# Hymba layer on one core: five of the up stage's 258-column tiles with rows 1280 bytes apart, and a down-stage pool that opens later

## The chip, the cores and the metric

The kernel runs on one core of a Trainium2 chip. A core has five engines with their own instruction streams: TensorE (PE in the profile; its weight loads are PEld), VectorE (DVE), ScalarE (ACT), GpSimd (POOL) and SyncE (SP), which here only issues DMA transfers. They share an on-chip memory of 128 partitions (SBUF); TensorE writes its sums to a second one (PSUM) in banks of 512 float32 columns. Engines wait for each other through semaphores.

The metric is device time of one execution in microseconds, the median of several runs. Lower is better.

## The reference

The reference is one decoder layer in float32: a normalized input goes through a joint projection into differential attention and an HGRN2 recurrence, an output projection and a residual sum, and then through a convolutional feed-forward block, which is what this change touches:

```python
D_FF = 2816
CONV_WIDTH = 3

def conv_ffn(a, w_up, conv_w, conv_b, w_down):
    u = a @ w_up                                   # (1040, 1024) @ (1024, 5632)
    C = u.shape[-1]
    u = lax.conv_general_dilated(
        u, conv_w[:, None, :].astype(u.dtype), window_strides=(1,),
        padding=[(CONV_WIDTH - 1, 0)], dimension_numbers=('NWC', 'WIO', 'NWC'),
        feature_group_count=C) + conv_b
    gate, up = jnp.split(u, 2, axis=-1)
    return (jax.nn.gelu(gate, approximate=True) * up) @ w_down

def reference(...):
    ...
    for l in range(DEPTH):
        ...
        mix = jnp.concatenate([y_diff, y_hgrn], axis=-1) @ w_out[l]
        h = h + rmsnorm(mix, ln_mix_post[l])
        a = rmsnorm(h, ln_ffn_pre[l])
        y = conv_ffn(a, w_ffn_up[l], ffn_conv_w[l], ffn_conv_b[l], w_ffn_down[l])
        h = h + rmsnorm(y, ln_ffn_post[l])
    return h[:, N_META:, :]
```

## The kernel before

**Precision.** Each float32 product is made of three matmuls in a rounded format (float32r): an operand is split into `hi`, its rounded value, and `lo`, the rest, and the matmuls are hi x hi, hi x lo and lo x hi. ScalarE makes `hi` (a CAST in the profile), VectorE or GpSimd subtract it from the operand to get `lo`.

**The up stage** computes u = a @ w_up transposed: channels on the partitions, tokens along the columns. The tokens lie in two parts, p = 0 and p = 1. With the halo of the convolution a part has 516 or 512 columns, which are handled as two halves of `WN[p]` = 258 or 256. The loop `for ft in range(1, NF)` goes over 21 blocks of 128 gate channels and the 128 up channels that belong to them; the prediction calls one pass a round. Block 0 is done ahead of it by `plain_unit`.

A round is a 2 x 2 by 2 x 2 block product (channels gate and up, halves of the inner dimension, halves of the tokens) in Winograd's form: seven products instead of eight, the steps j = 0 to 6. Product j multiplies a weight combination, made anew in every round by `prep` (names `uh`, `ul` for its hi and lo, `ws` for sums on GpSimd, `ra` for the loaded weights), with a token combination, made once before the loop (`t_sums`, `t_split`, `quarter`) and kept in a tile `t0_j` or `t1_j` (the profile calls all of them `t`). A tile holds eight rows per partition: four k-slices of hi, then four of lo. Before the change they follow each other without a gap: 258 x 4 = 1032 bytes for p = 0, 1024 for p = 1. All tiles start at an address that is 32 above a multiple of 64.

`unit(ft, p, ...)` is one part of a round, written as a generator that yields after each step. Step j issues twelve matmuls, for each k-slice hi x hi, then weight-hi x token-lo, then weight-lo x token-hi (lines 1383, 1384, 1385). The loop takes step j of p = 0, then of p = 1, then the next step. TensorE's order is exactly this. The products are added into three PSUM banks: `pa` for j = 0 and 4, `pb` for j = 1, 3 and 5, `pc` for j = 2 and 6. Between two products in one bank the sum so far is read out, by ScalarE (`x`, `ug`) or by VectorE (`u`, `uu`, `ug`), and the next product waits for that read. So j = 3 waits until VectorE has formed `u` (code name `u2`) from `pb`, and j = 5 until it has formed the next `u` (`u3`).

After the last step `gated` does the convolution: per side (gate `ug`, up `uu`) ScalarE starts it (`c` = last tap plus bias), VectorE adds two taps (SCALAR_TENSOR_TENSOR), ScalarE applies gelu to the gate, GpSimd multiplies the two sides, and SyncE stores the result to DRAM (`gsc`). These run while TensorE does the next round's first steps.

The other engines' order is set by a scheduler when the kernel is built, within what the code asks for (`issue_after`). Memory is handed out by pools: a tile of a pool with a tag takes the place of the last tile with that tag, and a pool opened later takes the addresses of pools closed before; the new user waits for the last readers of the tiles that lay there.

**The token tiles' places before.** For p = 0: tiles 0 and 4 in the pool `early` (`e0`, `e1`), tiles 1, 2, 3 in `tsplit`, tile 6 in the mix pool's X1, tile 7 (used by block 0 alone) in X2, and tile 5 after it in X2. For p = 1 they lie in `tsplit`, `tsplit2` and X0.

**The down stage** computes y = g @ w_down with the same Winograd form, 11 k-steps for each of seven products. `operands` loads a block of g (`gi`) and of the weights (`wi`), or uses the loaded ones it is given, and splits them into `gh`, `gl`, `wh`, `wl`. Twelve 512-column matmuls follow per k-step (`mms`). The buffers for `gi`, `gh` and `gl`, four of each, come from the pool `down`, which before is open from the start of the up loop. The first three k-steps are prepared early: in the last round, their loads are issued at j = 1 (after the store of the round before) and their splits at j = 4, 5, 6. When the up stage's pools are closed the pool `fin` takes their place.

Of the kernel before, what the change touches and what calls it, by code (L numbers as in the profile page):

```python
# [9 lines left out]
F32 = mybir.dt.float32  # L10
F32R = mybir.dt.float32r
# [6 lines left out]
P = 128  # L18
# [6 lines left out]
NF = DFF // P  # L25
# [7 lines left out]
C0 = [0, 514]  # L33
FA, FH, FO = 840, 800, 740


# [49 lines left out]
def layer_kernel(ctx: ExitStack, tc: tile.TileContext, x, meta, table, lbl, gpre, gpost, win,  # L86
# [1161 lines left out]
    def t_tiles(p, j, where, tag):  # L1248
        tag, n = (tag + (8 * WN[p],))[:2]
        both = where.tile([P, n], F32R, tag=tag, name=f"t{p}_{j}")[:, :8 * WN[p]].rearrange("p (a c) -> p a c", a=8)  # L1250
        return both[:, 0:4], both[:, 4:8]

    def t_split(p, j, src, where, *tag):
        hi, lo = t_tiles(p, j, where, tag)
        A.copy(hi, src)
        V.tensor_tensor(lo, src, hi.bitcast(F32), op=ALU.subtract)
        tt[p][j] = (hi, lo)
# [6 lines left out]
    def t_sums(p, where, last):  # L1264
# [4 lines left out]
        for j, b in ((1, b22), (2, b11), (3, b12)):  # L1269
            t_split(p, j, b, where, f"t{p}_{j}")  # L1270
        V.tensor_tensor(b21, b21, b22, op=ALU.subtract)
# [150 lines left out]
    t_split(1, 6, quarter(1, 6), mxp, "X0", MIX["X0"])  # L1422
    t_sums(0, tp, (mxp, "X2", MIX["X2"]))
    close(a_cms.pop())
    t2_cm, t2p = pool("tsplit2", 1)
    gap(t2p, "gap2", 320)
    p1 = plain_unit(1, ps_b)
# [6 lines left out]
    gap(cv, "gap3", 224)  # L1434
    dn_cm, dn = pool("down", 4, "right")
    next(p0)
    for j in range(4, 7):
        prep(7 + j)
# [8 lines left out]

    def g_in(k, half, nm):
        t = dn.tile([P, 512], F32, tag="gk", name=f"gi{nm}_{k}")
        SY.dma_start(t, g_src(k, half))  # L1450
        return t
# [10 lines left out]
    def operands(pr, k, loaded=None):  # L1462
# [20 lines left out]
        nm = f"{pr}_{k}"  # L1483
        gh = dn.tile([P, 512], F32R, tag="gh", name=f"gh{nm}")
        gl = dn.tile([P, 512], F32R, tag="gl", name=f"gl{nm}")
        split(gh, gl, a, V)
# [5 lines left out]
    for ft in range(1, NF):  # L1492
        units = [unit(ft, p, ps_b) for p in range(2)]
        for j in range(7):
            prep(7 * (ft + 1) + j)
            for u in units:
                next(u)
            if (ft, j) == (1, 1):
                with tc.issue_after(marks[1, 1].ins):
                    next(p1)  # L1500
            if ft == NF - 1 and j == 1:
                with tc.issue_after(marks["store"].ins):
                    opens = [(g_in(k, 0, "1"), w_in(1, k)) for k in range(LOOK)]
            if ft == NF - 1 and j > 3:
                with tc.issue_after(marks["left"].ins):
                    ready[j - 4] = operands(1, j - 4, opens[j - 4])
    close(t2_cm, t_cm, xu_cm, mx_cm)

# [186 lines left out]
```

## Time and profile before

| what | value |
|---|---|
| median of 3 runs | 1302.69 us (1301.43 to 1303.88) |
| profiled execution, its own time | 1300.73 us |
| its span, first to last instruction | 1298.9 us |
| granted TensorE clock, mean | 0.998 |
| TensorE busy | 1268.1 us, 98% of the span |
| VectorE, ScalarE, GpSimd busy | 68%, 54%, 37% |
| up loop, first matmul to last | 656.09 to 1076.39 us |
| down stage from | 1076.50 us |

In the profile an instruction stands with its line, its engine, the operation, what it writes and reads by the program's names (without buffer numbers), and its shape. Nearly all VectorE, ScalarE and GpSimd instructions have line 53, that of a helper through which they are issued. Matmuls overlap: one lasts some 280 ns from start to end while the next starts 113 to 125 ns after it, so the pace is read from the distance of starts, not from the durations. In the timeline a row is the start in microseconds, the duration, the engine, and the instruction; "x2" are several alike in a row; in brackets stands idle time of the engine before it and what ended it. A row of a stretch has the busy time and number of instructions of PE, PEld, DVE, ACT and POOL, the granted clock, the busy share of the DMA engines and GB/s. A row of the waits has who waited for whom, the sum in microseconds, the number of times and the longest.

### The profile page before, as it was taken

Reading aid. Unit: us, or ns where it says so; the run is one execution under the profiler, and the core shown is the slowest. Engines: PE = TensorE matmul, PEld = TensorE weight load, DVE = VectorE, ACT = ScalarE, POOL = GpSimd, SP = SyncE. Lnnn points to the kernel's source line nnn. Section 1 sums busy time; section 2 is a strip of 40 time slices with the busy share of each in tenths; the row PEclk is TensorE's granted clock in tenths of the full one; section 3 lists DMA queues with packets and bytes.
Section 4 is the critical chain, followed back from the end, with each engine's and each line's share of the span. In section 5 each row is a group of like instructions: output and inputs, shape, how many; then the busy total and the mean of one; then the engine's idle time right before and its main releaser. Section 6 shows DMA issues by size and latency. Waiting matters only on the chain.

```text
span 1298.9 us, 26100 instructions
## 1 busy us (share of the span) xinstructions
PE 1268.1 (98%) x10154; PEld 1179.0 (91%) x10154; DVE 887.0 (68%) x1488; ACT 695.1 (54%) x1639; POOL 482.6 (37%) x387
## 2 busy tenths in 40 slices
PE   8999999999999999999999999999999999999996
PEld 7999999899999998767899999999999998888885
DVE  7574646465645574547897877778778767697686
ACT  8465466546654764356854544544445435554553
POOL 5231423242323310353066575666665731010121
PEclk9999999999999999999999999999999999999999
DMA  6244655182644532787312222222222128964263
GB/s 215 94 99 89 120 120 116 47 156 78 125 116 86 122 103 90 222 272 265 117 67 82 90 75 82 74 89 83 74 75 90 66 79 274 336 203 170 90 211 122
DMA packets 116418, 165.04 MB, mean 127 GB/s; under 512 B 10099, under 2 KB 57523, under 8 KB 116294
## 3 DMA queue, kind: packets, MB, share of 16 engines
q1 hardware_dynamic: 93062, 151.84, 35.1%
q0 software_dynamic: 23232, 11.54, 7.6%
q8 instruction: 80, 1.31, 0.4%
q14 instruction: 44, 0.36, 0.1%
HBM read 134.24 MB, written 52.17 MB: 144 GB/s over the span
## 4 chain that ended last, share of the span: by engine, by line
PE 46%; DVE 4%; ACT 2%; issue 1%; DMA 1%; DVEq 0%; ACTq 0%
PE pd L1544 5%; PE pd L1545 5%; PE pd L1543 5%; PE pb L1383 5%; PE pb L1384 4%; PE pb L1385 4%; PE pa L1384 3%; PE pa L1383 3%; PE pa L1385 3%; PE pc L1384 3%; PE pc L1383 3%; PE pc L1385 3%; DVE c L53 1%; DVE t L53 1%; DVE xh L53 1%
## 5 line engine op out<-in xcount | busy, mean ns | idle before, releaser
L1383 PE MATMUL pb<-t,uh 128*128 128x258 f32 x504 | 142.5, 283 | 2.9 <-DVE u L53 2.7
L1384 PE MATMUL pb<-t,uh 128*128 128x258 f32 x504 | 141.2, 280 | 0.0
L1385 PE MATMUL pb<-t,ul 128*128 128x258 f32 x504 | 141.0, 280 | 0.0
L1544 PE MATMUL pd<-wl,gh 128*128 128x512 f32 x308 | 120.5, 391 | 2.0 <-DVE wl L53 2.0
L1545 PE MATMUL pd<-wh,gl 128*128 128x512 f32 x308 | 120.0, 390 | 0.0
L1543 PE MATMUL pd<-wh,gh 128*128 128x512 f32 x308 | 120.0, 390 | 0.0
L53 DVE SCALAR_TENSOR_TENSOR c<-uu,cwt,c 128x514 f32<-128x514 f32 (+1 forms) x88 | 96.5, 1096 | 19.6 <-ACT c L53 18.9
L53 POOL TENSOR_TENSOR c<-c,c 128x514 f32<-128x514 f32 (+1 forms) x44 | 63.8, 1449 | 122.3 <-ACT c L53 120.2
L1383 PEld LDWEIGHTS pb<-t,uh 128*128 128x128 f32 x504 | 95.0, 189 | 5.3 <-DVE u L53 5.3
L1385 PEld LDWEIGHTS pb<-t,ul 128*128 128x128 f32 x504 | 95.3, 189 | 0.0
L1384 PEld LDWEIGHTS pb<-t,uh 128*128 128x128 f32 x504 | 95.0, 188 | 0.0
L1384 PE MATMUL pa<-t,uh 128*128 128x258 f32 (+1 forms) x336 | 94.7, 282 | 0.0
L1383 PE MATMUL pa<-t,uh 128*128 128x258 f32 (+1 forms) x336 | 94.6, 281 | 0.0
L1385 PE MATMUL pa<-t,ul 128*128 128x258 f32 (+1 forms) x336 | 94.3, 281 | 0.0
L1384 PE MATMUL pc<-t,uh 128*128 128x258 f32 (+1 forms) x336 | 94.1, 280 | 0.0
L1385 PE MATMUL pc<-t,ul 128*128 128x258 f32 (+1 forms) x336 | 94.1, 280 | 0.0
L1383 PE MATMUL pc<-t,uh 128*128 128x258 f32 (+1 forms) x336 | 93.9, 279 | 0.0
L53 DVE SCALAR_TENSOR_TENSOR c<-ug,cwt,c 128x514 f32<-128x514 f32 (+1 forms) x88 | 88.3, 1004 | 1.4 <-ACT c L53 0.6
L53 ACT CAST uh<-ra 128x512 fp32r<-128x512 f32 x67 | 41.1, 617 | 63.2 <-PE pb L1384 42.0
L53 DVE TENSOR_TENSOR ul<-ra,uh 128x512 fp32r<-128x512 f32 x42 | 40.2, 957 | 48.7 <-ACT uh L53 48.7
L53 POOL TENSOR_TENSOR ul<-ws,uh 128x512 fp32r<-128x512 f32 x42 | 60.4, 1437 | 34.4 <-ACT uh L53 33.7
L1544 PEld LDWEIGHTS pd<-wl,gh 128*128 128x128 f32 x308 | 57.8, 188 | 15.5 <-DVE wl L53 3.7
(388 smaller groups left out, 4167.1 us busy)
## 6 DMA issues: line engine op xcount, KB each, us to landing
ra<-in_wup_dram SPq DMA_DIRECT2D x88, 256.0 KB, 2.6
mp<-msc SPq DMA_DIRECT2D x23, 512.0 KB, 5.0
tsc<-in_wdown_dram SPq DMA_DIRECT2D x44, 256.0 KB, 4.5
wi<-tsc SPq DMA_DIRECT2D x44, 256.0 KB, 2.7
gi<-gsc SPq DMA_DIRECT2D x33, 256.0 KB, 4.4
wi<-in_wdown_dram SPq DMA_DIRECT2D x33, 256.0 KB, 5.2
gsc<-c SPq DMA_DIRECT2D x22, 257.0 KB, 2.0
tsc<-in_wdown_dram POOLq DMA_DIRECT2D x22, 256.0 KB, 7.4
```

The lines of the kernel that those rows point to most:

```text
L53: ins = call(*args, **kw)
L1383: T.matmul(pt, hi[:, s], th[:, k], start=(first and k == 0), stop=False, skip_group_check=True)
L1384: T.matmul(pt, hi[:, s], tl[:, k], start=False, stop=False, skip_group_check=True)
L1385: T.matmul(pt, lo[:, s], th[:, k], start=False, stop=(k == 3), skip_group_check=True)
L1543: T.matmul(py, gh[:, s], wh, start=(k == 0 and pr not in (3, 7)), stop=False, skip_group_check=True)
L1544: T.matmul(py, gh[:, s], wl, start=False, stop=False, skip_group_check=True)
L1545: T.matmul(py, gl[:, s], wh, start=False, stop=(k == NH - 1), skip_group_check=True)
```

## The change

`wide_tiles` makes a token tile of 8 rows of `ROW` = 320 float32 values, 1280 bytes, of which 258 are used, from column `off` on. The tiles 1, 2, 3, 5 and 6 of p = 0 become such tiles; tile 3 starts 32 columns (128 bytes) into its rows and tile 6 starts 16 (64 bytes) in. Tiles 0, 4 and 7 of p = 0 and all of p = 1 keep their rows. Tile 5 no longer takes tile 7's place but has a tag of its own in `tsplit`. Tile 6 is made in X1 as before and copied by ScalarE into a wide tile of a new pool, `tsplit3`, after the last step of block 0.

A wide tile takes 10240 bytes per partition instead of 8256. The pool `down` no longer exists during the up stage; it is opened when the up stage's tiles are gone. The three early k-steps of the down stage therefore use other places: their g loads go to `raw_g`, which takes the place of p = 1's tile 0, and their `gh` and `gl` to four rows of 512 columns in a tile that takes the place of p = 0's wide tile 1 (two k-steps) or 2 (one).

```diff
+ROW = 320
...
+    def wide_tiles(j, off, where=None):
+        both = (where or tp).tile([P, 8 * ROW], F32R, tag=f"t0_{j}", name=f"t0_{j}w")
+        both = both.rearrange("p (a c) -> p a c", a=8)[:, :, off:off + WN[0]]
+        return both[:, 0:4], both[:, 4:8]
+
     def t_split(p, j, src, where, *tag):
-        hi, lo = t_tiles(p, j, where, tag)
+        hi, lo = wide_tiles(j, where) if isinstance(where, int) else t_tiles(p, j, where, tag)
         A.copy(hi, src)
         V.tensor_tensor(lo, src, hi.bitcast(F32), op=ALU.subtract)
...
         for j, b in ((1, b22), (2, b11), (3, b12)):
-            t_split(p, j, b, where, f"t{p}_{j}")
+            t_split(p, j, b, where[j] if p == 0 else where, f"t{p}_{j}")
...
-    t_sums(0, tp, (mxp, "X2", MIX["X2"]))
+    t_sums(0, {1: 0, 2: 0, 3: 32}, (0,))
     close(a_cms.pop())
     t2_cm, t2p = pool("tsplit2", 1)
-    gap(t2p, "gap2", 320)
...
-    dn_cm, dn = pool("down", 4, "right")
+    t3_cm, t3p = pool("tsplit3", 1)
     next(p0)
+    own, tt[0][6] = tt[0][6], wide_tiles(6, 16, t3p)
+    for new, old in zip(tt[0][6], own):
+        A.copy(new, old.bitcast(F32))
...
-    def g_in(k, half, nm):
-        t = dn.tile([P, 512], F32, tag="gk", name=f"gi{nm}_{k}")
+    def g_in(k, half, nm, t=None):
+        t = dn.tile([P, 512], F32, tag="gk", name=f"gi{nm}_{k}") if t is None else t
...
-        gh = dn.tile([P, 512], F32R, tag="gh", name=f"gh{nm}")
-        gl = dn.tile([P, 512], F32R, tag="gl", name=f"gl{nm}")
+        if loaded:
+            gh, gl = loaded[2:]
+        else:
+            gh = dn.tile([P, 512], F32R, tag="gh", name=f"gh{nm}")
+            gl = dn.tile([P, 512], F32R, tag="gl", name=f"gl{nm}")
...
             if ft == NF - 1 and j == 1:
+                raw_g = tp.tile([P, 4, 512], F32, tag="t1_0", name="raw_g")
                 with tc.issue_after(marks["store"].ins):
-                    opens = [(g_in(k, 0, "1"), w_in(1, k)) for k in range(LOOK)]
+                    opens = [(g_in(k, 0, "1", raw_g[:, k]), w_in(1, k)) for k in range(LOOK)]
+            if ft == NF - 1 and j in (4, 6):
+                halves = tp.tile([P, 8 * ROW], F32R, tag=f"t0_{j // 2 - 1}", name=f"open{j}")[:, 16:2064]
+                halves = halves.rearrange("p (a c) -> p a c", a=4)
             if ft == NF - 1 and j > 3:
+                a = 2 * (j % 2)
                 with tc.issue_after(marks["left"].ins):
-                    ready[j - 4] = operands(1, j - 4, opens[j - 4])
-    close(t2_cm, t_cm, xu_cm, mx_cm)
+                    ready[j - 4] = operands(1, j - 4, opens[j - 4] + (halves[:, a], halves[:, a + 1]))
+    close(t3_cm, t2_cm, t_cm, xu_cm, mx_cm)
+    dn_cm, dn = pool("down", 4, "right")
```

TensorE's order does not change. On the other engines only a few instructions move. ScalarE in round 1, before the change (`x1_1_0` and `x1_1_1` are the reads of `pa` for the two parts, `c0` and `c1` the convolutions' starts, `uh15` to `uh17` weight casts for the next steps):

```order
L53 COPY x1_1_0_8007<-pa1_0_8010 128x258
L53 ACTIVATE c0_0_0_7966<-ug0_0_7642,cbt_85,cwt_84 128x514
L53 ACTIVATE c1_0_0_7971<-uu0_0_7643,cbt_85,cwt_84 128x514
L53 COPY x1_1_1_8026<-pa1_1_8029 128x256
L53 CAST uh15_8045<-ws2_8043 128x512
L53 ACTIVATE c0_0_1_8077<-ug0_1_7819,cbt_85,cwt_84 128x510
L53 ACTIVATE c1_0_1_8082<-uu0_1_7820,cbt_85,cwt_84 128x510
L53 ACT_TABLE_LOAD
L53 ACTIVATE c0_0_0_7966<-c0_0_0_7966 128x514
L53 CAST uh16_8088<-ws1_7999 128x512
```

and after it:

```order
L54 COPY x1_1_0_8009<-pa1_0_8012 128x258
L54 ACTIVATE c0_0_0_7965<-ug0_0_7642,cbt_85,cwt_84 128x514
L54 ACTIVATE c1_0_0_7970<-uu0_0_7643,cbt_85,cwt_84 128x514
L54 CAST t0_6w_7976<-t0_6_7575 128x4x258 x2
L54 ACT_TABLE_LOAD
L54 ACTIVATE c0_0_0_7965<-c0_0_0_7965 128x514
L54 COPY x1_1_1_8028<-pa1_1_8031 128x256
L54 CAST uh15_8047<-ws2_8045 128x512
L54 ACTIVATE c0_0_1_8079<-ug0_1_7818,cbt_85,cwt_84 128x510
L54 ACTIVATE c1_0_1_8084<-uu0_1_7819,cbt_85,cwt_84 128x510
L54 CAST uh16_8090<-ws1_8001 128x512
```

The two copies (one row, x2), the table load and the gelu of p = 0 (the ACTIVATE that reads and writes `c0_0_0`) now stand ahead of `x1_1_1`, of `uh15` and of the convolution's start for p = 1.

VectorE at the same place, before the change (`u2_1_0` and `u2_1_1` read the bank that j = 3 waits for, `ul15` is the remainder of weight `uh15`):

```order
L53 SCALAR_TENSOR_TENSOR c1_0_0_7971<-uu0_0_7643,cwt_84,c1_0_0_7971 128x514
L53 TENSOR_TENSOR ul15_8046<-ws2_8043,uh15_8045 128x512
L53 TENSOR_TENSOR u2_1_0_8008<-pb1_0_8049,x1_1_0_8007 128x258
L53 TENSOR_TENSOR u2_1_1_8027<-pb1_1_8063,x1_1_1_8026 128x256
L53 SCALAR_TENSOR_TENSOR c0_0_1_8077<-ug0_1_7819,cwt_84,c0_0_1_8077 128x510
```

and after it:

```order
L54 SCALAR_TENSOR_TENSOR c1_0_0_7970<-uu0_0_7643,cwt_84,c1_0_0_7970 128x514
L54 TENSOR_TENSOR u2_1_0_8010<-pb1_0_8051,x1_1_0_8009 128x258
L54 TENSOR_TENSOR u2_1_1_8029<-pb1_1_8065,x1_1_1_8028 128x256
L54 TENSOR_TENSOR ul15_8048<-ws2_8045,uh15_8047 128x512
L54 SCALAR_TENSOR_TENSOR c0_0_1_8079<-ug0_1_7818,cwt_84,c0_0_1_8079 128x510
```

The weight's remainder has moved behind the two `u2`.

SyncE's queue in the last round and at the start of the down stage, before the change (`gi1_k` and `wi1_k` are the loads of k-step k of the first product, `gi5_11` belongs to a later product's sums, the last row is the store of the last round's p = 0):

```order
L1450 DMA gi1_2_13356<-gsc_90 128x512
L1459 DMA wi1_2_13358<-in_wdown_dram 128x512
L1450 DMA gi1_3_13556<-gsc_90 128x512
L1459 DMA wi1_3_13558<-in_wdown_dram 128x512
L1459 DMA wi1_4_13591<-in_wdown_dram 128x512
L1450 DMA gi5_11_13569<-gsc_90 128x512
L1459 DMA wi1_5_13615<-in_wdown_dram 128x512
L1450 DMA gi1_4_13589<-gsc_90 128x512
L1459 DMA wi1_6_13639<-in_wdown_dram 128x512
L1351 DMA gsc_90<-c0_21_0_13495 128x514
```

and after it:

```order
L1458 DMA raw_g_13350<-gsc_90 128x512
L1467 DMA wi1_2_13358<-in_wdown_dram 128x512
L1467 DMA wi1_3_13558<-in_wdown_dram 128x512
L1467 DMA wi1_4_13591<-in_wdown_dram 128x512
L1467 DMA wi1_5_13615<-in_wdown_dram 128x512
L1467 DMA wi1_6_13639<-in_wdown_dram 128x512
L1458 DMA gi1_3_13556<-gsc_90 128x512
L1458 DMA gi5_11_13569<-gsc_90 128x512
L1458 DMA gi1_4_13589<-gsc_90 128x512
L1458 DMA gi1_5_13613<-gsc_90 128x512
L1357 DMA gsc_90<-c0_21_0_13492 128x514
```

The load of `gi1_3` now stands behind the weight loads up to `wi1_6`, and `gi1_5` has come ahead of the store.

## The prediction

> **What bounds the kernel now.** I read the page's head first, then busy time by stretch, then the timeline of TensorE and of VectorE over a few rounds of the up stage, then the waits. A round is one pass of the `ft` loop: seven steps j, each twice (p = 0 with 258 columns, p = 1 with 256), twelve matmuls a group.
>
> ```profile
> span 1298.9 us, 26100 instructions
> PE 1268.1 (98%) x10154; PEld 1179.0 (91%) x10154; DVE 887.0 (68%) x1488; ACT 695.1 (54%) x1639; POOL 482.6 (37%) x387
> ```
> ```profile
> 680.00:1060.00 380.00, 379.79 (x3214) 377.83 (x3214) 291.75 (x423) 183.00 (x326) 239.93 (x169) 1.00 0.22 77
> ```
>
> The second row is the steady part of the up stage: TensorE is never idle for more than moments, at a granted clock of 1.00, and VectorE is busy 77%. So a round lasts as long as its matmuls, unless someone keeps them waiting. These are first matmuls of groups in round 4 (start, duration); two neighbouring starts are the two ends of one group:
>
> ```profile
> 738.90 0.29 PE L1383 MATMUL pa<-t,uh 128*128 128x258 f32 x1
> ...
> 741.72 0.28 PE L1383 MATMUL pb<-t,uh 128*128 128x258 f32 x1
> ...
> 743.16 0.28 PE L1383 MATMUL pb<-t,uh 128*128 128x256 f32 x1
> ...
> 744.57 0.28 PE L1383 MATMUL pc<-t,uh 128*128 128x258 f32 x1
> ...
> 745.99 0.28 PE L1383 MATMUL pc<-t,uh 128*128 128x256 f32 x1
> ...
> 747.35 0.28 PE L1383 MATMUL pb<-t,uh 128*128 128x258 f32 x1
> ...
> 748.78 0.28 PE L1383 MATMUL pb<-t,uh 128*128 128x256 f32 x1
> ...
> 752.99 0.28 PE L1383 MATMUL pb<-t,uh 128*128 128x258 f32 x1
> ...
> 754.41 0.28 PE L1383 MATMUL pb<-t,uh 128*128 128x256 f32 x1
> ...
> 755.77 0.28 PE L1383 MATMUL pc<-t,uh 128*128 128x258 f32 x1
> ...
> 757.24 0.28 PE L1383 MATMUL pc<-t,uh 128*128 128x256 f32 x1
> ...
> 758.61 0.29 PE L1383 MATMUL pa<-t,uh 128*128 128x258 f32 x1
> ```
>
> The round takes 19.71 us. The 258-column groups of the five tiles in question take 1.44 (j = 1), 1.42 (j = 2), 1.43 (j = 3), 1.42 (j = 5) and 1.47 (j = 6), 7.18 together. The 256-column groups take 1.36 (j = 2 and 5) or 1.37 (j = 6), but 1.41 after tile 1. At 1.36, 113 ns a matmul, 258 columns would cost 1.36 x 258/256 = 1.37. So the 258-column groups lose 0.05 to 0.10 us each to something other than their two extra columns. What sets them apart in the code is that their rows start at every multiple of 8 bytes (1032 apart), while the 256-column rows are 1024 apart. That the same kind of 256-column group takes 1.36 or 1.41 shows a second factor: a group seems to inherit a slow or a fast pace from the one before.
>
> Every second round also has a wait at j = 3, where matmuls add into a bank that VectorE must first have read:
>
> ```profile
> 727.49 0.39 PE L1383 MATMUL pb<-t,uh 128*128 128x258 f32 x1
> ```
> ```profile
> 766.95 0.28 PE L1385 MATMUL pc<-t,ul 128*128 128x256 f32 x1
> 767.23 0.39 PE L1383 MATMUL pb<-t,uh 128*128 128x258 f32 x1
> 767.45 0.29 PE L1384 MATMUL pb<-t,uh 128*128 128x258 f32 x1
> ```
> ```profile
> PEld pb L1383 <- DVE u L53: 2.2, 10, 0.2
> ```
>
> Ten such waits; the steps 0.28 and 0.22 instead of 0.11 and 0.12 cost 0.27 us each, of which 0.10 is the restart. Two rounds so take 39.72 or so (19.86 on average) instead of 39.4. The VectorE rows of that loop:
>
> ```profile
> 734.01 0.88 DVE L53 TENSOR_TENSOR ul<-ra,uh 128x512 fp32r<-128x512 f32 x1 [2.50 <-ACT uh L53]
> 734.90 0.43 DVE L53 TENSOR_TENSOR uu<-pb,x 128x258 f32<-128x258 f32 x1
> ...
> 746.38 0.74 DVE L53 TENSOR_TENSOR u<-pb,x 128x258 f32<-128x258 f32 x2
> ...
> 753.73 1.63 DVE L53 TENSOR_TENSOR ul<-ra,uh 128x512 fp32r<-128x512 f32 x1 [2.45 <-ACT uh L53]
> 755.29 0.41 DVE L53 TENSOR_TENSOR uu<-pb,x 128x258 f32<-128x258 f32 x1
> ```
> ```profile
> 753.53 1.29 POOL L53 TENSOR_TENSOR ul<-ra,uh 128x512 fp32r<-128x512 f32 x1
> ```
>
> From `uu` (it opens the convolutions) to the `u` that frees the bank VectorE works nearly without a break: 755.29 to the matmul at 767.23 is 11.94. Before that lies the leg from j = 3 to `uu`. In round 4 it is 747.35 to 755.29, 7.94, because `ul` took 1.63 beside a GpSimd `ul`. In round 3 `ul` took 0.88; its `uu` plus 11.94 gives 746.84, and TensorE came at 747.35, so nobody waited.
>
> **The change, part by part.** *Wide rows.* Five tiles times 12 matmuls per round. No instruction is added in the round. Bounds: at best all five groups run at 1.37, saving 7.18 - 6.85 = 0.33, and the 256-column group after tile 1 goes from 1.41 to 1.36: 0.38 in all, a TensorE round of 19.33. At worst they run at the slow pace, 1.41 x 258/256 = 1.42, and pass it on (a rival, below). I take the best end: these rows become like the 256-column ones, all starting at the same remainder, and four of the seven groups of that kind in round 4 are at the fast pace after a neighbour that isn't.
>
> The Trainium skill, page "TensorE: Matmul & The Clock Gate", section "Wait — 56ns, not 53.3ns?", has warm back-to-back matmuls start every N / 2.4 GHz plus about 2.5 ns: 109 ns for 256 columns and 110 for 258, whatever the rows' distance. This trace disagrees, with 113 to 122 ns; by that rule the wide rows would save nothing.
>
> *What VectorE leaves of it.* Of the leg, the p = 0 groups j = 3 and j = 5 shrink by 0.06 and 0.05. A round with a quick `ul` then needs 7.41 (727.49 to 734.90) - 0.11 + 11.94 = 19.24: just under TensorE's 19.33. With a slow `ul` it needs 7.94 - 0.11 + 11.94 = 19.77. Slow every second round as now: (19.33 + 0.10 restart + 19.77)/2 = 19.60, a gain of 0.27 against 19.87. Every third: (19.43 + 19.33 + 19.77)/3 = 19.51, 0.36. Never: 0.54. Always: 0.10. The quick rounds now have 0.09 of slack instead of 0.51, so `ul` comes earlier against GpSimd's and hits it less often: I take between every second and every third, 0.31. Over 20 rounds (2 to 21) that is 6.2 us.
>
> *Round 1.* It is VectorE's, not TensorE's:
>
> ```profile
> PE pb L1383 <- DVE u L53: 2.7, 2, 1.4
> ```
> ```profile
> 641.75 2.97 ACT L53 CAST t<-at 128x1032 fp32r<-128x1032 f32 x3
> ...
> 660.08 0.35 ACT L53 COPY x<-pa 128x256 f32<-128x256 f32 x1
> ...
> 664.35 0.63 ACT L53 ACTIVATE c<-c 128x514 f32<-128x514 f32 x1 [0.68 <-DVE c L53]
> ```
> ```profile
> 665.51 0.74 DVE L53 TENSOR_TENSOR u<-pb,x 128x258 f32<-128x258 f32 x2
> 666.18 1.11 DVE L53 SCALAR_TENSOR_TENSOR c<-ug,cwt,c 128x510 f32<-128x510 f32 x1
> ...
> 672.89 0.41 DVE L53 TENSOR_TENSOR u<-pb,x 128x258 f32<-128x258 f32 x1
> ```
>
> So its faster groups gain nothing. The two copies of tile 6 take 1.0 each (2.97 for three). They, the table load and the gelu now stand ahead of `x` and of the second pair's convolution starts on ScalarE. The gelu still waits for VectorE until 664.3, so `x` comes at 664.9 instead of 660.1, the next weight cast ends at 665.8 and the convolution start at 666.6. VectorE's `u` for p = 0 moves ahead of a weight remainder and ends the first wait somewhat sooner, but the convolution begins at 666.6 for 666.18, and at its end stands the `u` at 672.89 for which TensorE waits: +0.4. Bounds: -0.6 (all GpSimd work that slows these convolutions moves away) to +1.0. Tile 6 is needed at j = 6, two groups after 672.89: hidden. Tile 5's own buffer ends a wait for tile 7 that no row shows: nothing.
>
> *The start of the down stage.* The first three operands lie in buffers of p = 1's tile 0 and p = 0's tiles 1 and 2, last read at j = 0, 1 and 2 of the round, before the loads and splits. The fourth load moves behind four weight loads on the queue:
>
> ```profile
> 1068.08 0.43 SPq L1450 DMA_DIRECT2D gi<-gsc  x1
> ...
> 1075.26 0.33 SPq L1459 DMA_DIRECT2D wi<-in_wdown_dram  x1
> ```
> ```profile
> gi<-gsc SPq DMA_DIRECT2D x33, 256.0 KB, 4.4
> ```
> ```profile
> 1079.44 0.64 ACT L53 ACTIVATE c<-c 128x514 f32<-128x514 f32 x1 [0.92 <-DVE c L53]
> ```
> ```profile
> 1082.96 0.68 DVE L53 TENSOR_TENSOR wl<-wi,wh 128x512 fp32r<-128x512 f32 x1
> ```
> ```profile
> 1083.69 0.50 PE L1544 MATMUL pd<-wl,gh 128*128 128x512 f32 x1 [1.34 <-DVE wl L53]
> ```
>
> It is issued after the 1075.26 row instead of at 1068.08 and lands near 1080.1. Its cast now stands ahead of the last round's first gelu, which slips by about 1.2, and with it a product and a store whose rows are read much later. Its remainder on VectorE comes after the 1082.96 row as before, so TensorE resumes at 1083.69 for the same reason. I count nothing; the cover is the 3 us from 1080.1 to 1083. If it is gone, +1.3.
>
> *Sum.* -6.2 + 0.4 = -5.8. The profiled execution took 1300.73 (span 1298.9), 1.96 under the median 1302.69, a little below the lowest shown; the difference carries over: 1302.7 - 5.8 = 1296.9.
>
> **The rivals.** *All of it kept.* No slow `ul` left: 20 x 0.54 - 0.4 = 10.4, 1292.3. For it: less slack. Against it: it needs GpSimd never in the way.
>
> *VectorE takes over.* Every round slow: 20 x 0.10 - 0.4 = 1.6, 1301.1. For it: 77% busy, and TensorE's rest shrinks. Against it: a stalled round has had a quick `ul` after it (734.01).
>
> *The slow pace spreads* (the other side). The five wide groups take 1.42, saving 0.08, and the five 256-column groups now at 1.36 or 1.37 take 1.41, losing 0.23: 0.15 x 20 + 0.4 = 3.4 more, 1306.1. For it: the 256-column group after tile 1 stays at 1.41 for all twelve matmuls though its rows never shift, so equal rows alone don't end the slow pace. Against it: the same kind of group at j = 2 and 5 is quick. It decides once two more groups a round turn slow with nothing saved elsewhere.
>
> *Nothing in the matmuls changes.* The rows' distance is not the cause; only round 1's 0.4 is left: 1303.1. The page's rule above would have it so. Against it: 1.47 for tile 6 beside 1.37 for its neighbour, which two columns don't explain.
>
> **How the numbers follow.** The forecast (1295 to 1299) 0.60, all kept 0.10, VectorE 0.10, slow pace 0.13, nothing 0.07. The time is that of the first, 1296.9. The range leaves out the slow pace and some of the ends: 1291.8 to 1303.2. About 0.2% (2.6 us) is what a measurement of this kernel can tell from no change: faster 0.73 (the first two and a third of the VectorE case), same 0.13, slower 0.14.
>
> **What would show it.** Right: the five 258-column groups at 1.37 to 1.38, the 256-column group after tile 1 at 1.36, the pace of tiles 0 and 4 unchanged, a round near 19.5, waits on `u` at j = 3 no rarer than one round in three; round 1's second wait up by 0.4; the fourth operand landing near three microseconds before its remainder starts. Wrong: groups of 1.42, or quick groups with a round still near 19.8, the rest being waits on `u`.

## The result, and the profile after

The changed kernel took 1304.38 us (median of 22 runs), the kernel before, run beside it, 1302.07 us (22 runs). The ratio is 1.0028 with a 95% interval of 1.0015 to 1.0041: slower by some 3.6 us (the ratio goes by the means, 1305.9 and 1302.1; the medians lie 2.3 apart), where 5.8 us less were forecast. The 22 times fall in two groups, 13 from 1301.1 to 1305.4 (mean 1303.3) and nine from 1307.6 to 1311.3 (mean 1309.6). No run of the kernel before is above 1306. The profiled execution, 1310.75 us by its own time, is one of the long ones, 10.0 us longer than the profiled one of before.

These rows cut the kernel before at the first up matmul, at the starts of rounds 2 and 18, and at the last up matmul (stretch and its length, then busy time and instructions of PE, PEld, DVE, ACT and POOL, the granted clock, the DMA share, GB/s):

```profile
656.09:679.10 23.01, 20.29 (x171) 19.89 (x169) 21.71 (x25) 12.90 (x22) 20.03 (x11) 1.00 0.23 81
679.10:997.04 317.94, 317.79 (x2690) 316.22 (x2689) 243.81 (x353) 152.81 (x273) 205.07 (x144) 1.00 0.23 81
997.04:1076.39 79.35, 79.29 (x673) 78.90 (x672) 58.03 (x90) 37.62 (x69) 38.32 (x27) 1.00 0.27 89
1076.39:1298.90 222.51, 210.99 (x927) 173.11 (x925) 167.29 (x243) 109.94 (x220) 26.71 (x17) 0.99 0.58 198
```

And the changed kernel at the same places:

```profile
658.86:683.71 24.85, 21.73 (x170) 21.34 (x169) 23.05 (x26) 15.01 (x24) 20.31 (x12) 0.93 0.25 85
683.71:1002.05 318.34, 318.15 (x2690) 317.02 (x2689) 243.97 (x353) 152.86 (x272) 204.93 (x145) 1.00 0.24 80
1002.05:1081.23 79.18, 79.18 (x674) 79.06 (x672) 57.90 (x89) 37.91 (x68) 37.55 (x27) 1.00 0.25 81
1081.23:1308.90 227.67, 213.49 (x927) 174.07 (x925) 165.79 (x243) 109.72 (x220) 31.63 (x17) 0.98 0.59 197
```

Between the two spans (1298.9 and 1308.9) lie 2.8 us ahead of the up stage, 1.8 in round 1, 0.4 in the sixteen rounds after it, -0.2 in the last four, and 5.2 in the down stage. The 2.8 arise ahead of 400 us, in code that the change leaves alone, and three executions of the changed kernel start their first up matmul at 656.6, 658.9 and 659.7 us (e11, this one and e10 below), so they say nothing of the change. The steady round, where the gain was to be, went from 317.94/16 = 19.87 to 318.34/16 = 19.90 us.

**The matmuls.** The starts of the groups in round 4 of the changed kernel, a round without a wait; `t_1w` to `t_6w` are the wide tiles:

```profile
726.25 0.28 PE L1389 MATMUL pb<-t_1w,uh 128*128 128x258 f32 x1
...
727.69 0.28 PE L1389 MATMUL pb<-t,uh 128*128 128x256 f32 x1
...
729.06 0.28 PE L1389 MATMUL pc<-t_2w,uh 128*128 128x258 f32 x1
...
730.51 0.28 PE L1389 MATMUL pc<-t,uh 128*128 128x256 f32 x1
...
731.88 0.28 PE L1389 MATMUL pb<-t_3w,uh 128*128 128x258 f32 x1
...
733.30 0.28 PE L1389 MATMUL pb<-t,uh 128*128 128x256 f32 x1
...
737.52 0.28 PE L1389 MATMUL pb<-t_5w,uh 128*128 128x258 f32 x1
...
738.97 0.29 PE L1389 MATMUL pb<-t,uh 128*128 128x256 f32 x1
...
740.36 0.28 PE L1389 MATMUL pc<-t_6w,uh 128*128 128x258 f32 x1
...
741.79 0.28 PE L1389 MATMUL pc<-t,uh 128*128 128x256 f32 x1
...
743.21 0.28 PE L1389 MATMUL pa<-t,uh 128*128 128x258 f32 x1
```

The wide groups take 1.44, 1.45, 1.42, 1.45 and 1.43 us, 7.19 together, where they took 7.18 with narrow rows. Single groups did move: tiles 2 and 5 lost 0.03 each and tile 6 gained 0.04. Inside tile 1's group the steps between matmuls still vary, from 114 to 125 ns as before, although every row now starts at the same remainder; tile 6's group settles at an even 120 ns after its fifth matmul. The 256-column group after tile 1 did turn quick (1.41 to 1.37), but the one after tile 6 turned slow (1.37 to 1.42). TensorE's round without a wait went from 19.71 to 19.77.

**Round 1.** TensorE's waits between 655 and 690 us (who waited for whom, the sum, the number, the longest):

```profile
PE pb L1389 <- DVE u L54: 3.1, 2, 2.4
```

Before, it was 2.7 in two waits of at most 1.4. So the sum rose by 0.4 and the longest by 1.0. These are the reads of `pb` that end the two waits, on VectorE:

```profile
667.68 0.79 DVE L54 TENSOR_TENSOR u<-pb,x 128x258 f32<-128x258 f32 x2
...
676.05 0.74 DVE L54 TENSOR_TENSOR u<-pb,x 128x258 f32<-128x258 f32 x2
```

They start 8.37 us apart, before the change 7.38 (665.51 to 672.89), and the weight's remainder that moved now stands between them: the first wait became shorter, the second longer. In the stretch row of round 1 the granted clock is 0.93 instead of 1.00: right behind the long wait, from 676.6 to 679.6 us, it is 0.50, and the matmuls start 214 ns apart instead of 119.

**The start of the down stage.** The last round's two gate products on GpSimd, before and after the change:

```profile
1080.15 1.74 POOL L53 TENSOR_TENSOR c<-c,c 128x514 f32<-128x514 f32 x1 [15.33 <-ACT c L53]
1083.23 1.55 POOL L53 TENSOR_TENSOR c<-c,c 128x510 f32<-128x510 f32 x1 [1.34 <-issue]
```
```profile
1085.42 8.42 POOL L54 TENSOR_TENSOR c<-c,c 128x514 f32<-128x514 f32 x2 [15.82 <-ACT c L54]
```

The gelu ahead of the first of them, and what follows in the changed kernel on SyncE's queue, on ScalarE, on TensorE, and its row in the waits between 1080 and 1112 us:

```profile
1084.71 0.63 ACT L54 ACTIVATE c<-c 128x514 f32<-128x514 f32 x1
```

```profile
1080.45 1.81 SPq L1458 DMA_DIRECT2D gi<-gsc  x4
1092.16 0.32 SPq L1357 DMA_DIRECT2D gsc<-c  x1
...
1093.86 0.32 SPq L1357 DMA_DIRECT2D gsc<-c  x1
1094.29 0.88 SPq L1458 DMA_DIRECT2D gi<-gsc  x2
```
```profile
1097.49 0.62 ACT L54 CAST gh<-gi 128x512 fp32r<-128x512 f32 x1 [6.58 <-DMA gi<-gsc]
...
1104.40 1.32 ACT L54 CAST gh<-gi 128x512 fp32r<-128x512 f32 x2 [5.77 <-DMA gi<-gsc]
```
```profile
1105.07 0.50 PE L1560 MATMUL pd<-wh,gh 128*128 128x512 f32 x1 [3.62 <-ACT gh L54]
```
```profile
PE pd L1560 <- ACT gh L54: 3.6, 1, 3.6
```

The two products are done only at about 1092 and 1093.8. The stores of their rows stand on the queue ahead of the next g loads, so SyncE issued nothing from 1082.3 to 1092.2. The first of these loads went out at 1094.3, ScalarE waited 6.6 and 5.8 us for g loads, and TensorE 3.6 us for ScalarE. After that wait, too, matmuls start 427 ns apart instead of 227 for some 3 us.

### The profile page after: what moved, and what is told of

The parts are those of the page before. It is cut to its first block, busy times and chain, and to the rows that moved or that the text cites. A ratio compares the mean times of both kernels' runs of the same rounds, so it can differ in the third digit from the quotient of the medians.

```text
span 1308.9 us, 26099 instructions
## 1 busy us (share of the span) xinstructions
PE 1273.9 (97%) x10154; PEld 1183.8 (90%) x10154; DVE 887.0 (68%) x1488; ACT 697.4 (53%) x1641; POOL 485.7 (37%) x387
## 4 chain that ended last, share of the span: by engine, by line
PE 79%; DVE 8%; ACT 4%; DMA 4%; issue 2%; SPq 0%; POOL 0%; DVEq 0%; ACTq 0%; POOLq 0%
PE pd L1561 5%; PE pd L1562 4%; PE pb L1389 4%; PE pd L1560 4%; PE pb L1390 4%; PE pb L1391 4%; PE pa L1389 3%; PE pa L1390 3%; PE pa L1391 3%; PE pc L1390 3%; PE pc L1391 3%; PE pc L1389 3%; PE pa L740 3%; PE pi_hf L242 1%; DMA ra<-in_wup_dram 1%
## 5 line engine op out<-in xcount | busy, mean ns | idle before, releaser
L1560 PE MATMUL pd<-wh,gh 128*128 128x512 f32 x296 | 116.1, 392 | 3.6 <-ACT gh L54 3.6
L1561 PE MATMUL pd<-wl,gh 128*128 128x512 f32 x296 | 116.4, 393 | 0.7 <-DVE wl L54 0.6
L54 POOL TENSOR_TENSOR c<-c,c 128x514 f32<-128x514 f32 (+1 forms) x44 | 68.6, 1561 | 120.7 <-ACT c L54 119.4
L1389 PE MATMUL pb<-t,uh 128*128 128x256 f32 x252 | 70.4, 279 | 0.0
L1560 PEld LDWEIGHTS pd<-wh,gh 128*128 128x128 f32 x296 | 56.1, 189 | 15.9 <-ACT gh L54 4.3
L1390 PE MATMUL pb<-t,uh 128*128 128x256 f32 x252 | 70.0, 278 | 0.0
L1391 PE MATMUL pb<-t,ul 128*128 128x256 f32 x252 | 69.9, 277 | 0.0
L1562 PEld LDWEIGHTS pd<-wh,gl 128*128 128x128 f32 x296 | 56.0, 189 | 12.3 <-DVE gl L54 0.9
L54 POOL TENSOR_TENSOR ws<-ra,ra 128x512 f32<-128x512 f32 x42 | 61.9, 1473 | 7.3 <-DMA ra<-in_wup_dram 4.0
L1391 PEld LDWEIGHTS pa<-t,ul 128*128 128x128 f32 x336 | 63.8, 190 | 0.0
L1390 PEld LDWEIGHTS pa<-t,uh 128*128 128x128 f32 x336 | 63.5, 189 | 0.0
L1389 PEld LDWEIGHTS pa<-t,uh 128*128 128x128 f32 x336 | 63.4, 189 | 0.0
```

The lines of the kernel that those rows point to most:

```text
L54: ins = call(*args, **kw)
L1389: T.matmul(pt, hi[:, s], th[:, k], start=(first and k == 0), stop=False, skip_group_check=True)
L1390: T.matmul(pt, hi[:, s], tl[:, k], start=False, stop=False, skip_group_check=True)
L1391: T.matmul(pt, lo[:, s], th[:, k], start=False, stop=(k == 3), skip_group_check=True)
L1560: T.matmul(py, gh[:, s], wh, start=(k == 0 and pr not in (3, 7)), stop=False, skip_group_check=True)
L1561: T.matmul(py, gh[:, s], wl, start=False, stop=False, skip_group_check=True)
```

## The experiments

All are made from the changed kernel; ratios are to the kernel before, run on the same chip.

**Rows narrow again, all else as changed (e1).**

```diff
-ROW = 320
+ROW = 258
...
-    t_sums(0, {1: 0, 2: 0, 3: 32}, (0,))
+    t_sums(0, {1: 0, 2: 0, 3: 0}, (0,))
...
-    own, tt[0][6] = tt[0][6], wide_tiles(6, 16, t3p)
+    own, tt[0][6] = tt[0][6], wide_tiles(6, 0, t3p)
```

> The changed kernel with all five tiles at 258-column rows again (1032 bytes apart, offsets 0), and the late pool, the copy of tile 6 and everything else left as changed. Theory A (the distance of the rows does nothing; the loss sits where the down stage opens and in round 1): round length stays 19.9 us, the five p=0 groups of tiles 1, 2, 3, 5, 6 stay at 119 to 123 ns a matmul, the wait on gh of about 3.6 us in the down stage is still there, time 1302 to 1306, that is 1.001 to 1.004 of the kernel before. Rival B (wide rows themselves cost or gain in the matmuls): the round moves by more than 0.1 us and the time with it by more than 2 us.

Ratio 1.0028 (1.0015 to 1.0041), 1306.14 us, the same as with wide rows, and the same two groups of times (six runs to 1305.2, six from 1307.1). The round is 19.89, and from the last up matmul to the end it takes 227.6 us. The waits in round 1 and at the start of the down stage:

```profile
PE pb L1389 <- DVE u L54: 2.8, 2, 1.5
```
```profile
PE pd L1560 <- ACT gh L54: 3.7, 1, 3.7
PE pd L1561 <- DVE wl L54: 0.3, 1, 0.3
```

Theory A holds: over a round the rows' distance neither gains nor costs (tile 2 is back at 1.42 us, tile 5 takes 1.46, and tile 6 has its 1.43 with narrow rows too), and the wait on `gh` comes without it. Round 1 has its waits of before back although the two copies of tile 6 are still there: with narrow rows VectorE's order at that place is the one of before (`ul15` ahead of the two `u2`), and ScalarE starts the convolution of p = 1 ahead of its table load again.

**Rows 1536 bytes apart for tiles 1 and 2, narrow for 3, 5 and 6 (e7).**

```diff
-        both = (where or tp).tile([P, 8 * ROW], F32R, tag=f"t0_{j}", name=f"t0_{j}w")
+        both = (where or tp).tile([P, 8 * (ROW if j < 3 else WN[0])], F32R, tag=f"t0_{j}", name=f"t0_{j}w")
...
-ROW = 320
+ROW = 384
...
```

> The changed kernel with the rows of tiles 1 and 2 1536 bytes apart (three times 512, so that all rows of a tile start at the same place within 512 bytes, as those of the 256-column tiles do) and those of tiles 3, 5 and 6 1032 bytes apart. Theory A (rows do nothing to 258-column matmuls): tiles 1 and 2 stay at 119 to 121 ns, round 19.9 us, time 1302 to 1309. Rival D (1280 was the wrong distance: the place within 512 bytes counts): tiles 1 and 2 go at 114 to 115 ns, TensorE's round 0.13 us shorter.

The groups of tiles 1 and 2 take 1.444 and 1.448 us (median of 16 rounds), 120 ns a matmul, against 1.433 and 1.418 before the change; round 19.92. So 1280 was not merely the wrong distance. The time (1309.33, two runs) has the long wait on `gh` in it and tells nothing more.

**256 of the 258 columns, wide rows (e5) and narrow rows (e6).**

```diff
             for k in range(4):
+                w = n if first and k == 0 else 256
...
-                T.matmul(pt, hi[:, s], th[:, k], start=(first and k == 0), stop=False, skip_group_check=True)
-                T.matmul(pt, hi[:, s], tl[:, k], start=False, stop=False, skip_group_check=True)
-                T.matmul(pt, lo[:, s], th[:, k], start=False, stop=(k == 3), skip_group_check=True)
+                T.matmul(pt[:, :w], hi[:, s], th[:, k, :w], start=(first and k == 0), stop=False, skip_group_check=True)
+                T.matmul(pt[:, :256], hi[:, s], tl[:, k, :256], start=False, stop=False, skip_group_check=True)
+                T.matmul(pt[:, :256], lo[:, s], th[:, k, :256], start=False, stop=(k == 3), skip_group_check=True)
```

> The changed kernel (wide rows), with the p=0 matmuls of rounds 1 to 21 over 256 of their 258 columns; only the first matmul of each of the three groups that open a bank stays at 258. It leaves out the last two columns of each half, so part of the up product is missing from it. Theory A (the pace follows the number of columns: 258 goes at 119 to 123 ns wherever its rows start, 256 at 113.4): the p=0 groups fall from 1.44 to about 1.37 us, TensorE's round from 19.71 to 19.2, and the time shows what VectorE leaves of it: between 2 us less (VectorE's slow loop of 19.77) and 12 us less (its quick loop of 19.24). Rival B (the pace follows the rows or the group before, not the count): p=0 groups stay at 118 or above, time within 2 us of the changed kernel.

> As the run before (256 of 258 columns in the p=0 matmuls, two columns of each half left out), but with rows 1032 bytes apart in all tiles. Theory A (number of columns alone): the same 113 to 114 ns a matmul as with wide rows, the same round and time within 1 us. Rival C (with a whole number of 64-byte pieces in a row the row's start counts after all): 117 to 120 ns here against 113 to 114 with wide rows, a round 0.3 to 0.5 us longer than there.

Starts of tile 2's group and its successor, and of tile 5's, in round 4 with wide rows:

```profile
726.49 0.28 PE L1390 MATMUL pc<-t_2w,uh 128*128 128x258 f32 x1
...
727.87 0.28 PE L1390 MATMUL pc<-t,uh 128*128 128x256 f32 x1
...
734.83 0.28 PE L1390 MATMUL pb<-t_5w,uh 128*128 128x256 f32 x1
...
736.19 0.28 PE L1390 MATMUL pb<-t,uh 128*128 128x256 f32 x1
```

And of tile 2's group with narrow rows:

```profile
726.17 0.28 PE L1390 MATMUL pc<-t_2w,uh 128*128 128x258 f32 x1
...
727.62 0.28 PE L1390 MATMUL pc<-t,uh 128*128 128x256 f32 x1
```

With 256 columns in wide rows, tile 5's group takes 1.36 us, twelve even steps of 113 ns, and tile 2's 1.38, at 113 after its first three matmuls. Tiles 1 and 3 go at an even 118 (1.41), tile 6 at 113 to 121 (1.42). With 256 columns in narrow rows all five stay uneven, at 119 to 121 on average, 1.45 for tile 2. So in these runs a quick group took both, 256 columns and rows that start alike, and even then three of five are slow. Neither Theory A (the count alone) nor Rival B of e5 (the rows or the neighbour alone) holds; Rival C of e6 is nearest, though the shortest round with narrow rows, 19.73, is only 0.24 longer than with wide ones. The time with narrow rows was 1307.66 us (four runs, 1.0049, 1.0036 to 1.0063), with waits on `gh` of 3.7 us in its profile.

The time with wide rows, 1304.46 us (1.0014, 0.9998 to 1.0031; the times run from 1296.3 to 1307.9), again holds the long wait on `gh` in its profile. The round shows what VectorE leaves of faster matmuls. TensorE's shortest round fell from 19.77 to 19.49, by 0.28, but the mean only from 19.90 to 19.72, by 0.18: the wait at j = 3 grew. The waits of TensorE's weight loads in rounds 2 to 17, here and in the changed kernel:

```profile
PEld pb L1390 <- DVE u L54: 3.0, 6, 0.6
```
```profile
PEld pb L1389 <- DVE u L54: 0.9, 4, 0.4
```

**More columns than needed in the wide tiles (e9)**, on top of the stores of e2 below.

```diff
+W = {1: 264, 2: 272, 3: 260, 5: 264, 6: 260}
...
-        both = both.rearrange("p (a c) -> p a c", a=8)[:, :, off:off + WN[0]]
+        both = both.rearrange("p (a c) -> p a c", a=8)[:, :, off:off + W[j]]
+        G.memset(both[:, :, WN[0]:].bitcast(F32), 0.0)
...
+            w = W.get(j, n) if p == 0 else n
...
-                T.matmul(pt, hi[:, s], th[:, k], start=(first and k == 0), stop=False, skip_group_check=True)
+                T.matmul(pt[:, :w], hi[:, s], th[:, k], start=(first and k == 0), stop=False, skip_group_check=True)
```

> The changed kernel with the last round's stores on GpSimd's queue, and the matmuls of the five wide tiles over more columns than are needed (zeros behind the 258): 264 for tiles 1 and 5, 272 for tile 2, 260 for tiles 3 and 6. Nothing is left out. Both the 256-column groups and the 512-column ones cost 0.443 ns a column at their quick pace and some 4.5 ns a matmul more at their slow one; 258 columns in wide rows were uneven, 114 to 125 ns. Theory A (uneven because a row of 258 does not end on a whole piece; 260, 264 or 272 columns do): the matmuls of a group become even, at 115.1 or 119.6 ns (260), 116.9 or 121.4 (264), 120.4 or 125 (272), and the count at which they do tells how large the piece is. Rival B (only 256 columns, that is rows of 1024 bytes, run even): they stay uneven, 118 to 127 ns in one group. Time by A between 1300 and 1303, by B 1303 to 1307, because the matmuls do more columns for nothing.

1304.66 us, ratio 1.0015 (1.0003 to 1.0026), which is in Rival B's range. Group times by tile: 1.47 (264, tile 1), 1.48 (272, tile 2), 1.44 (260, tile 3), 1.46 (264, tile 5), 1.42 (260, tile 6). In tiles 1, 3 and 5 the steps settle at an even 120 ns after three to eight matmuls, for 260 and 264 columns alike; tile 2's stay within 122 and 125 after the third. So 260 and 264 columns mostly run even, as Theory A has it, but none at the quick pace that it allowed for. No extra column pays for itself here.

**The last round's stores on GpSimd's queue (e2).**

```diff
-        marks["store"] = SY.dma_start(gsc[P * ft: P * (ft + 1), C0[p]:C0[p] + 2 * WN[p] - 2], cg)
+        marks["store"] = (G if ft == NF - 1 else SY).dma_start(gsc[P * ft: P * (ft + 1), C0[p]:C0[p] + 2 * WN[p] - 2], cg)
```

> The changed kernel with the last round's two stores of gated rows issued from GpSimd's own queue instead of SyncE's; the slow product stays. Theory A (the loads gi1_6, gi1_7 wait on SyncE's queue behind a store that waits for a slow GpSimd product): the product still takes 6 us or more beside VectorE's remainders, but the loads go out at once, the waits of ScalarE's gh on gi of 6.58 and 5.77 us fall under 2 us, TensorE's wait of 3.6 us on gh and the half clock behind it go, last up matmul to end of span falls from 227.65 to about 222.5 us, time about 4 us less, 1299.5 to 1301.5 (0.998 to 1.000 of before). Rival B (the loads are late through their own transfer of 4 to 5 us or through the four buffers of the later pool): the wait at that place stays above 2 us and the time at 1303 to 1305.

1303.03 us, ratio 1.0008 (0.9999 to 1.0016); none of the 12 runs is above 1304.8. From the last up matmul to the end it takes 222.8 us instead of 227.7, and the one wait left at that place is not on `gh`:

```profile
PE pd L1561 <- DVE wl L54: 1.3, 1, 1.3
```

That fits Theory A, but the time is 1.5 us above its range, and in this profile the products were quick, which it had not expected, so the run does not separate the two halves of the mechanism:

```profile
1084.17 1.41 POOL L54 TENSOR_TENSOR c<-c,c 128x514 f32<-128x514 f32 x1 [15.65 <-ACT c L54]
```

**The same with narrow rows (e8)** does, by luck.

> The changed kernel with rows 1032 bytes apart in all five tiles (round 1 then has the waits of the kernel before, 1.4 and 1.7 us) and the last round's stores on GpSimd's queue (no wait on gh in the down stage). Theory A (these two places hold the whole loss): up stage 420.5 us from first to last matmul, 222.7 from there to the end, time as the kernel before, ratio 0.999 to 1.0005. Rival E (the copy of tile 6, the later pool or the moved loads cost something else): ratio 1.001 or more.

1301.56 us, ratio 0.9997 (0.9988 to 1.0006). The first product was slow here, and it cost nothing, since no load stood behind its store (GpSimd's row, and the stretch from the last up matmul to the end):

```profile
1083.81 6.73 POOL L54 TENSOR_TENSOR c<-c,c 128x514 f32<-128x514 f32 x1 [15.79 <-ACT c L54]
```
```profile
1079.61:1301.80 222.19, 211.53 (x927) 172.92 (x925) 167.47 (x243) 109.77 (x220) 32.67 (x19) 0.99 0.61 201
```

This kernel still has the copy of tile 6, the later pool and the moved loads, and nothing of the loss is left. e1 is the same kernel but for the stores: with products as slow it took 227.6 us in this stretch and 1.0028 of the time before. So the loads behind the stores hold the loss of e1, the whole of it as far as the runs can tell.

**The last round's products on VectorE (e3).**

```diff
-        G.tensor_tensor(cg, cg, cu, op=ALU.mult)
+        (V if ft == NF - 1 else G).tensor_tensor(cg, cg, cu, op=ALU.mult)
```

> The changed kernel with the last round's two gate products on VectorE instead of GpSimd, the stores left on SyncE's queue. Theory A (a GpSimd product is stretched from 1.6 us to over 6 because VectorE works without a gap beside it): on VectorE the two products take 0.6 to 1.2 us each, the stores go out 6 to 8 us earlier, the 3.6 us wait on gh goes, VectorE gives up about 2 us that it has no slack for at the start of the down stage, so the wait of 0.5 us there grows by up to 1.5 us: time 1300 to 1302.5. Rival B (as in the run with the stores on GpSimd's queue): the wait on gh stays over 2 us, time 1303 to 1306.

1303.92 us, ratio 1.0011 (1.0001 to 1.0021). Both products take 0.70 us on VectorE; the waits at the start of the down stage:

```profile
PE pd L1561 <- DVE wl L54: 0.9, 1, 0.9
PE pd L1560 <- ACT gh L54: 0.2, 1, 0.2
```

Theory A: with the product off GpSimd the stores go out at 1084.7 and 1087.6 and the loads behind them in time. The time came out 1.4 us above what I expected. Its profile keeps the waits of round 1 (3.2 us), but without the fall of the clock, and this round is only 0.5 us longer than before; the rest is not explained.

**No copy of tile 6 (e4)**, four wide tiles.

```diff
-    own, tt[0][6] = tt[0][6], wide_tiles(6, 16, t3p)
-    for new, old in zip(tt[0][6], own):
-        A.copy(new, old.bitcast(F32))
```

> The changed kernel without the copy of tile 6 (tile 6 stays where it was, 258-column rows; four wide tiles). Theory A (the copies stand ahead of x and of the convolution's starts on ScalarE in round 1 and lengthen one wait there to 2.6 us, behind which the clock is halved for 3.4 us): the two waits of round 1 come back to 1.4 and 1.6 us, no halved clock there, tile 6's matmuls go from 120 to 123 ns and the p=1 group behind it from 118 to 113.5 ns, which cancel; time 2 us less than the changed kernel, 1301.5 to 1303. Rival B (the wait of round 1 comes from the order of VectorE's work, not from the copies): the wait stays above 2.3 us and the time at 1303.5 to 1305.

1307.83 us (five runs), ratio 1.0044 (1.0031 to 1.0056): worse, against both theories. Round 1 has its waits of before (2.7, two, longest 1.4) and a clock of 1.00, as Theory A has it. But the load of `gi1_3` goes out at 1069.5 us, and the scheduler puts its cast ahead of a read of `pa` in the last round. (Presumably the copy's tile lay where the later pool's buffers will be, and without it they are free early; no run shows the places.) ScalarE, and TensorE's waits from 1075 to 1112 us:

```profile
1075.65 0.62 ACT L54 CAST gh<-gi 128x512 fp32r<-128x512 f32 x1 [4.97 <-DMA gi<-gsc]
```
```profile
PE pd L1558 <- DVE wl L54: 4.8, 2, 4.5
```

ScalarE stood 5 us for a transfer, everything behind it slipped, and TensorE waited 4.5 us in its third k-step. What the copy itself costs is not told by this run; e1 and e8 say that it is little.

**The changed kernel again, twice (e10, e11)**, for a profile of a short execution.

> The changed kernel itself, once more, for the profile of another execution: its times fall in two groups, 1301.1 to 1305.4 and 1307.6 to 1311.3. Theory A (the groups differ in whether GpSimd's two last gate products get through beside VectorE's unbroken run of remainders): an execution under 1305.5 shows products of 1.3 to 1.8 us, a VectorE remainder beside each stretched to 1.7 or more, and no wait of TensorE on gh above 1 us in the down stage; one over 1307 shows a product of 6 us or more and a wait over 3 us. Rival F (the groups come from another place, such as the clock in round 1 or ahead of the up stage): the products and the wait on gh look the same in both.

> The changed kernel itself, once more, as the run before: by theory A products of 1.3 to 1.8 us and no wait on gh over 1 us if this execution is under 1305.5 us, a product of 6 us or more and a wait over 3 us if it is over 1307; by rival F no such difference.

Both executions were long (1312.48 and 1307.49 us), with products of 8.1 and 8.4 us for the two and waits on `gh` of at most 3.9 and 2.9 us (over 3 was expected). Of the 5.0 us between them 3.1 lie ahead of the up stage and 1.4 in round 1, so the places that Rival F names make the spread inside a group. They don't make the groups: e11 has the early start and the unhalved clock, and with the slow products it is still as long as the shortest of the long runs. No profile of a short one was seen. That the short ones are those in which the products get through is argued from e2, e3 and e8, which break the chain at the store or at the product and have no run above 1306.6 (e9, with the same stores and longer matmuls, has one of 1307.1); it isn't shown directly.

## Why the prediction was wrong

*Wide rows: the step that failed.* I took the best end, 1.37 us a group, because the 256-column groups differ from the 258-column ones in the distance of rows. They differ in the number of columns too, and I set that aside by scaling a group's time by 258/256. The five groups sum to 7.19 us, not 6.85, and the term of -6.2 us came out as a round of 19.90 instead of 19.87. With 258 columns the distance gained nothing over a round (e1, e7); with 256 it did (e5 against e6). What in 258 columns keeps a group from the quick pace stays open. The second sign that I used, the slow 256-column group after tile 1, did turn quick as forecast (0.04 gained), and the one after tile 6 turned slow. The two don't hang together: in e4 both are quick, in e1 both slow. And one more group of 256 columns, the one after tile 4, took 1.42 us all along, which the prediction did not list. What sets such a group's pace I did not know, so a sum over single groups could not hold. Of my rivals, "nothing in the matmuls changes", at 0.07, is what the matmuls did. The rule of the Trainium skill that stood beside it (page "TensorE: Matmul & The Clock Gate", section "Wait — 56ns, not 53.3ns?") would likewise have saved nothing; the 109 to 110 ns a matmul that are worked out from it, an estimate, agree with none of the 113 to 125 measured.

*What VectorE leaves of it.* There was nothing to leave. e5, where TensorE's round did fall by 0.28, kept 0.18, two thirds; I had 0.31 of 0.38. The mechanism, a growing wait on `u` at j = 3, was right, and its size on the high side. (The pair of rounds ahead of it adds up to 39.69, 39.4 and 0.27, not 39.72; the gains were counted from the measured 19.87, so nothing hangs on it.)

*Round 1.* +0.4 was forecast for the waits, and their sum rose by 0.4. That the number fits is luck: the second wait alone was to grow by 0.4, and it grew by 1.0 (1.4 to 2.4 us) while the first shrank by 0.6. What I missed besides is that the clock is halved behind the long one: the round became 1.84 us longer. e10 and e11 price the clock: with the same waits round 1 took 24.89 us where it fell and 23.48 where it did not. What round 1 is worth in the runs is not settled: e8, which has its old waits back, is 0.1% below e2, which has not (0.9997 against 1.0008, with intervals that overlap), but e1 is no faster than the changed kernel (1.0028 both).

*Start of the down stage.* I had the mechanism up to the last link. The gelu was to slip by 1.2 us and with it "a product and a store whose rows are read much later". Counted from the last up matmul it slipped by 0.4 (3.05 us behind it before, 3.48 now). The fourth load landed in time, as forecast: TensorE's wait there, 1.34 us before, was 0.2:

```profile
PE pd L1561 <- DVE wl L54: 0.2, 1, 0.2
```

But behind that store on SyncE's queue stand the next g loads, whose rows have nothing to do with it, and the product could be kept out by nine VectorE instructions in a row and take several times as long. Zero was forecast, 5.2 us came in the profiled execution. In the runs it is about 2.6 us on average: the nine long runs of 22 are 6.3 us longer than the others, and e2, whose 12 runs have none of them, is 0.2% below the changed kernel.

*The other terms* held: TensorE's order, tiles 0 and 4, and the 256-column group after tile 1.

## What to carry to other kernels

Before a change of memory layout is priced from two kinds of instruction that differ in it, list what else sets them apart, and where the difference can be removed cheaply (two columns left out, here) measure it first. When an instruction slips, follow the queue that its store sits in, not only the readers of what it stores: a load that needs nothing from it can stand behind it. And one long wait can cost more than two short ones of the same sum, if the clock falls behind it.

## What was not expected of the hardware

*The clock can fall after a wait of 2.4 us.* After TensorE waits of 2.4 to 4.5 us, matmuls started 214 instead of 119 ns apart (256 and 258 columns) or 427 instead of 227 (512 columns) for about 3 us, in 14 of 16 such waits in round 1 and at the start of the down stage. After waits of up to 1.5 us at these two places it happened in no case. The two waits without it were of 2.5 us, in round 1 of e3 and e11, while others of 2.4 and 2.5 us had it, so the length alone does not decide there.

*GpSimd can be kept out by VectorE.* A product of 514 columns that takes 1.3 to 1.8 us took 6.7 in e8, and the two together 7.5 to 8.4 in seven other profiles. VectorE's instructions beside it then keep their time, one starting every 0.6 us; here are some of the changed kernel:

```profile
1086.08 0.68 DVE L54 TENSOR_TENSOR open<-raw_g,open 128x512 fp32r<-128x512 f32 x1
...
1087.28 0.68 DVE L54 TENSOR_TENSOR gl<-gi,gh 128x512 fp32r<-128x512 f32 x1
...
1089.69 0.69 DVE L54 TENSOR_TENSOR gl<-gi,gh 128x512 fp32r<-128x512 f32 x1
1090.29 2.39 DVE L54 TENSOR_TENSOR wl<-wi,wh 128x512 fp32r<-128x512 f32 x2
```

The last two together take 2.39 us, where two such took 1.28 in e2: there the first product gets through. Where the product was quick, one VectorE instruction beside it took 1.75 to 1.79 us instead of 0.68 or 0.74 (before the change, e2, e4, e9). It looks as if one of the two waits for the other. The Trainium skill, page "SBUF — State Buffer", section "Who interferes with whom", says that a VectorE instruction with two inputs in SBUF contends with a GpSimd instruction that reads SBUF, that the ports they share are an exclusive lock, and that the order of issue decides who blocks. The trace agrees where a single instruction is held up (1.79 us instead of 0.74); that a GpSimd instruction stays out over a run of nine VectorE instructions, for 5 us, the section does not say. VectorE's lack of gaps does not decide it: it worked without one beside the quick products of before and of e2 too. What decides between the two outcomes was not settled.

*The pace of a matmul group.* After their first few matmuls, groups of 256 columns run at an even 113 or an even 118 ns a matmul, and the tile alone does not decide which: e5 has all tiles where the changed kernel has them and differs in the p = 0 matmuls' columns only, yet the group after tile 1 goes at 118 there and at 113 in the changed kernel, the one after tile 6 at 113 there and at 118 in the changed kernel. A kernel gives the same pattern in each round, and in a second execution. What sets the pace stays open.
